# Key and query products stored once per direction, with a triangle cleared for each, in one layer of a gated DeltaNet and neighbourhood attention kernel

## The chip, the cores and the metric

The kernel runs on one core of one Trainium2 chip. The metric is the device time of one execution in microseconds (us). The engines are named as the profile names them: PE (TensorE matmul), PEld (its weight loads), DVE (VectorE), ACT (ScalarE), POOL (GpSimd) and SP (SyncE, which here issues the DMAs). Each has one instruction queue that it works through in order.

## The reference, cut to what matters

One layer: modulation, a combined input projection, a gated DeltaNet over 1280 tokens (256 of context, 1024 latent, 4 heads of 128), scanned once forward and once backward, beside a neighbourhood attention, an output projection and a SwiGLU. The part that the change concerns is what the scans need within a chunk:

```
gam = jnp.cumsum(g.astype(f32).reshape(B, H, n, CHUNK), axis=-1)
tril = jnp.tril(jnp.ones((CHUNK, CHUNK), dtype=bool))
strict = jnp.tril(jnp.ones((CHUNK, CHUNK), dtype=bool), -1)
decay = jnp.exp(jnp.where(tril, gam[..., :, None] - gam[..., None, :], -jnp.inf))
kb = k * beta[..., None]
m = jnp.where(strict, jnp.einsum("bhncd,bhnmd->bhncm", kb, k) * decay, 0.0)
...
qk = jnp.where(tril, jnp.einsum("bhncd,bhnmd->bhncm", q, k) * decay, 0.0)
...
o_b, S_b = chunk_gated_delta_rule(rev(q), rev(k), rev(v), rev(g[1]), rev(beta[1]), S0_b)
```

The products of keys with keys and of queries with keys are multiplied by a decay that holds in one triangle only: the lower one forward, the other one backward.

## The kernel before

The kernel works in chunks of 128 tokens: `NCH` = 10 chunks, of which the first two are context. It has stages one after the other: modulation from `wa` and the norms; the column blocks of the input projection (k, z, the attention's q, k and v, then v, z and q of the DeltaNet); in the middle of these the preparation of the scans; the scans and the attention; the output projection; and the FFN, whose 700 us (810 to the end) have nothing to do with the change.

A column block (class `Block`) is projected in three partial matmuls (L419: `hh,whi`, `hl,whi`, `hh,wlo`), convolved on DVE (L461 or L475) and normalised. Its method `finish` then makes the products. For k block i (head i) PE multiplies keys by keys, chunk by chunk, into PSUM, ACT copies them into the tile `kk` (L568, 128x1280), POOL multiplies `kk` by the identity into `kd` (L572), DVE sums that to the squared norms `SV` (L574), and POOL moves the 32x32 diagonal blocks out of `kk` (L577) and clears them (L578). SP then stores `kk` to `kk_d` in HBM (L580). For q block i `kT` is loaded back into `kTh`, PE multiplies it by the queries, ACT copies the products into a `kk` of 128x1024, and SP stores it to `qk_d`. `kk`, `kd`, `kTh` and the `vt` that holds a transposed block share one ring of three buffers (tag "kx"); ACT can fill one only when its earlier content is no longer needed.

The decays: DVE makes the tables (`decay_tables`: L806 to L840, ending in `G` and its halves `GH`, `GL`); PE takes sums over them (L848), which the later preparation (L871 on POOL, L884 on PE) needs too. It stands in DVE's queue around the fourth k block. In the preparation (`preps`, with `fetch` and `prep`), which runs beside the later column blocks, there are 10 iterations of two tiles each, one for each direction `d`. `fetch` loads `kk` from `kk_d`, and for latent chunks `at` from `qk_d`. POOL multiplies `GH` and `GL` by a triangle (L994, `rg`); PE sums these in a matmul with a triangle of ones, `mr[:, d]` (L1006); then a third matmul (L1009) of an identity `mr[:, 4]` with `mneg` adds −1e30 outside the triangle, so that ACT's exponential (L1014, `e`) is 0 there. DVE multiplies `kk` by `e` (L1017) and `at` by `e` (L1022); PE multiplies `kk` by the blocks `fx` (L1030), ACT copies, and then rounds of L1041 on PE with copies of `y` (L1043) follow.

The order of the instructions on the engines is set by a scheduler from the written program; some rows are kept in program order (L1008). The L223 matmuls sum the modulation products `acc`, which DVE accumulates in L238 from tiles `wad`.

## Time and profile before

| | us |
|---|---|
| median of 3 runs | 1509.69 (1507.06 to 1513.23) |
| the profiled execution | 1510.77 |
| its span | 1509.0 |
| PE busy | 1458.9 (97%) |
| DVE busy | 993.4 (66%) |
| ACT busy | 704.0 (47%) |
| POOL busy | 237.5 (16%) |
| mean granted TensorE clock | 0.996 |

A row of the timeline gives the start in us, the time that it takes (in a row with x2 or more, of all of them together), the engine, the line, the operation, what it writes and reads, and in brackets how long the engine sat idle before it and on what. A row of the groups gives the number, the busy time and the mean in ns. DMAs appear under SPq with the time that they take to issue; "landing" is the time from issue until the data has arrived.

### The profile page before, as it was taken

Reading aid. Unit: us, or ns where it says so; the run is one execution under the profiler, and the core shown is the slowest. Engines: PE = TensorE matmul, PEld = TensorE weight load, DVE = VectorE, ACT = ScalarE, POOL = GpSimd, SP = SyncE. Lnnn points to the kernel's source line nnn. Section 1 sums busy time; section 2 is a strip of 40 time slices with the busy share of each in tenths; the row PEclk is TensorE's granted clock in tenths of the full one; section 3 lists DMA queues with packets and bytes.
Section 4 is the critical chain, followed back from the end, with each engine's and each line's share of the span. In section 5 each row is a group of like instructions: output and inputs, shape, how many; then the busy total and the mean of one; then the engine's idle time right before and its main releaser. Section 6 shows DMA issues by size and latency. Waiting matters only on the chain.

```text
span 1509.0 us, 23906 instructions
## 1 busy us (share of the span) xinstructions
PE 1458.9 (97%) x8702; PEld 1222.2 (81%) x8702; DVE 993.4 (66%) x1716; ACT 704.0 (47%) x1389; POOL 237.5 (16%) x286
## 2 busy tenths in 40 slices
PE   6999999999999998999999999999999999999998
PEld 3788797877788887888878888888888888888887
DVE  5773589865463745779867489765555567598652
ACT  5443442456663246667843284333333334354440
POOL 1154501455652201112210000000000000000000
PEclk9999999999999999999999999999999999999999
DMA  9274132778665558999539205333333335798742
GB/s 385 79 220 138 57 83 64 248 211 248 189 195 185 157 164 289 300 261 293 166 119 338 76 28 174 134 105 105 105 105 105 105 105 174 271 349 279 251 140 84
DMA packets 205398, 267.36 MB, mean 177 GB/s; under 512 B 15968, under 2 KB 113760, under 8 KB 204256
## 3 DMA queue, kind: packets, MB, share of 16 engines
q1 hardware_dynamic: 197680, 260.01, 53.5%
q10 hardware_dynamic: 7600, 5.81, 1.2%
q8 instruction: 69, 1.13, 0.3%
q14 instruction: 49, 0.40, 0.1%
HBM read 201.02 MB, written 68.94 MB: 179 GB/s over the span
## 4 chain that ended last, share of the span: by engine, by line
PE 51%; ACT 1%; DVE 1%; issue 0%; DVEq 0%
PE ps L1404 28%; PE ps L1747 14%; PE ps L1533 3%; PE ps L1381 1%; PE ps L1555 1%; PE sc L322 1%; PE sc L332 1%; PE sc L309 1%; DVE bt L313 0%; ACT sq L1308 0%; PE ps L1258 0%; ACT oacc L1325 0%; PE ps L223 0%; PE ps L1279 0%; PE ps L1284 0%
## 5 line engine op out<-in xcount | busy, mean ns | idle before, releaser
L1465 ACT CAST uhi<-wq 128x512 fp32r<-128x512 f32 x101 | 61.3, 622 | 135.4 <-issue 84.6
L419 PE MATMUL blk<-hh,whi 128*128 128x512 f32 (+1 forms) x410 | 121.2, 389 | 1.5 <-ACT kk L568 1.4
L1465 ACT CAST uhi<-ws 128x512 fp32r<-128x512 f32 x91 | 53.9, 621 | 146.6 <-PE ps L1404 92.1
L615 PE MATMUL blk<-zw,hh 128*128 128x256 f32 (+1 forms) x576 | 113.2, 291 | 1.0 <-ACT cr L467 1.0
L419 PE MATMUL blk<-hl,whi 128*128 128x512 f32 (+1 forms) x410 | 113.4, 370 | 0.3 <-DVE hl L735 0.3
L419 PE MATMUL blk<-hh,wlo 128*128 128x512 f32 (+1 forms) x410 | 112.5, 371 | 0.6 <-POOL wlo L204 0.6
L1466 DVE TENSOR_TENSOR ulo<-wq,uhi 128x512 fp32r<-128x512 f32 x101 | 67.6, 687 | 59.1 <-ACT uhi L1465 32.8
L1404 PE MATMUL ps<-hT,uhi 128*128 128x512 f32 x336 | 103.7, 390 | 0.0
L1404 PE MATMUL ps<-lT,uhi 128*128 128x512 f32 x336 | 103.5, 389 | 0.0
L1404 PE MATMUL ps<-hT,ulo 128*128 128x512 f32 x336 | 103.4, 389 | 0.0
L615 PEld LDWEIGHTS blk<-zw,hh 128*128 128x128 f32 x576 | 91.5, 190 | 4.2 <-ACT cr L467 1.4
L1404 PE MATMUL ps<-hB,uhi 128*128 128x512 f32 x288 | 89.1, 390 | 0.0
L1404 PE MATMUL ps<-lB,uhi 128*128 128x512 f32 x288 | 88.8, 389 | 0.0
L1404 PE MATMUL ps<-hB,ulo 128*128 128x512 f32 x288 | 88.6, 389 | 0.0
L419 PEld LDWEIGHTS blk<-hh,wlo 128*128 128x128 f32 x410 | 71.2, 189 | 14.8 <-POOL wlo L204 0.9
L419 PEld LDWEIGHTS blk<-hl,whi 128*128 128x128 f32 x410 | 71.3, 189 | 14.3 <-DVE hl L735 0.8
L615 PE MATMUL blk<-zw,hl 128*128 128x256 f32 (+1 forms) x288 | 82.3, 286 | 0.0
L419 PEld LDWEIGHTS blk<-hh,whi 128*128 128x128 f32 x410 | 67.9, 190 | 16.7 <-issue 3.8
L204 POOL TENSOR_TENSOR wlo<-wraw,whi 128x1024 fp32r<-128x1024 f32 x18 | 44.8, 2491 | 185.1 <-ACT whi L203 178.8
L1404 PEld LDWEIGHTS ps<-lT,uhi 128*128 128x128 f32 x336 | 63.1, 188 | 13.2
L1404 PEld LDWEIGHTS ps<-hT,ulo 128*128 128x128 f32 x336 | 63.1, 188 | 13.1
L1404 PEld LDWEIGHTS ps<-hT,uhi 128*128 128x128 f32 x336 | 62.9, 188 | 12.9
(361 smaller groups left out, 3499.3 us busy)
## 6 DMA issues: line engine op xcount, KB each, us to landing
wq<-w_fo SPq DMA_DIRECT2D x99, 256.0 KB, 4.4
wq<-w_gu SPq DMA_DIRECT2D x88, 256.0 KB, 2.9
wad<-wa SPq DMA_DIRECT2D x64, 256.0 KB, 4.2
bt<-rpb SPq DMA_DIRECT2D x64, 192.0 KB, 4.0
t_d<-g SPq DMA_DIRECT2D x22, 512.0 KB, 3.5
fr<-t_d SPq DMA_DIRECT2D x44, 256.0 KB, 4.9
f_d<-g SPq DMA_DIRECT2D x33, 256.0 KB, 2.1
fr<-f_d SPq DMA_DIRECT2D x33, 256.0 KB, 4.4
```

The source lines that it names most:

```text
L204: lo_engine.tensor_tensor(o, r, h.bitcast(F32), OP.subtract)
L309: s = pe.matmul(sc[:, u * 640 + n0:u * 640 + n1], q, ks[i], start=i == 0, stop=i == 1)
L322: pe.transpose(sc[:, u * 640 + j * 128:u * 640 + (j + 1) * 128], bt[:, j * 128:(j + 1) * 128], ident)
L332: return pe.matmul(sc[u * ND:u * ND + ND, 1280:1408], vv, pts[u][:, j * 128:(j + 1) * 128], start=j == 0, stop=j == 4)
L419: pe.matmul(o, ww[:, k], xx[k][:, s], start=k == 0 and j == 0, stop=k == KT - 1 and j == 2)
L615: pe.matmul(p[:, :c1 - c0], x[k][:, s], ww[:, k, c0:c1], start=k == 0 and j == 0, stop=k == KT - 1 and j == 2)
L1381: pe.matmul(o, w[wi][:, k], parts[xi][k][:, s], start=k == 4 and j == 0, stop=k == 3 and j == 2)
L1404: pe.matmul(o, w[wi][:, k], x[xi][:, k], start=first and k == 0 and j == 0, stop=k == n - 1 and j == 2, skip_group_check=True)
L1465: act.copy(hi, self.raw[key])
L1466: dve.tensor_tensor(lo, self.raw[key], hi.bitcast(F32), OP.subtract)
L1533: pe.matmul(o, w[wi][:, k], parts[xi][k][:, s], start=k == 0 and j == 0, stop=k == KT - 1 and j == 2)
L1747: pe.matmul(o[b], w[wi][:, b], F[xn, p][xi], start=n in (0, 1, 5) and p == 0 and j == 0, stop=p == NFB // 2 - 1 and j == 2, skip_group_che ...
```

## The change

After the products of a block, DVE makes two masked copies of `kk`, one for each direction: `kk` times the triangle `M[C_LE + d]` into the tile that is free by then (`kd` for k, `kTh` for q), and then into `kk` itself. SP stores both, in HBM tensors with a leading dimension of 2 for the direction, and `fetch` loads those of its direction, as many bytes as before. With the products cleared outside the triangle, the third matmul of a preparation tile (L1009) goes, and with it `mneg` and the fifth slice of `mr`. That is 20 matmuls and 3 ACT operations less, 16 DVE multiplies and 8 stores of 640 or 512 KB more.

```diff
-    mr = const("mr", [128, 5, 128], F32R)
+    mr = const("mr", [128, 4, 128], F32R)
...
-    kk_d = dram.tile([128, NCH, 4, 128], F32, name="kk_d", tag="kk_d")
-    qk_d = dram.tile([128, 8, 4, 128], F32, name="qk_d", tag="qk_d")
+    kk_d = dram.tile([2, 128, NCH, 4, 128], F32, name="kk_d", tag="kk_d")
+    qk_d = dram.tile([2, 128, 8, 4, 128], F32, name="qk_d", tag="qk_d")
...
                     dst = kk_d if kind == "k" else qk_d
-                    sp.dma_start(dst[:, :, i], kk[:, c0:])
+                    other = kd if kind == "k" else kT.rearrange("p (c t) -> p c t", t=128)
+                    for d, x in enumerate((other, kk)):
+                        keep = M[C_LE + d].rearrange("p (o i) -> p o i", o=1).to_broadcast([128, NCH - c0, 128])
+                        dve.tensor_tensor(x[:, c0:], kk[:, c0:], keep, OP.mult)
+                        sp.dma_start(dst[d, :, :, i], x[:, c0:])
...
-                        act.copy(mr[:, 4], ident)
...
-        mneg = adp.tile([128, 2, 128], F32R, name="mneg", tag="mneg")
-        for d in range(2):
-            act.mul(mneg[:, d], mr[:, d].bitcast(F32), -1.0e30)
...
-                        sp.dma_start(kk, kk_d[:, c])
+                        sp.dma_start(kk, kk_d[d, :, c])
...
-                            sp.dma_start(at, qk_d[:, c - 2])
+                            sp.dma_start(at, qk_d[d, :, c - 2])
...
-                            m = pe.matmul(p, mr[:, d], fl(rgs[2 * d + j]), start=j == 0, stop=False)
+                            m = pe.matmul(p, mr[:, d], fl(rgs[2 * d + j]), start=j == 0, stop=j == 1)
                             if i == 0:
                                 tc.keep_in_program_order(m)
-                        pe.matmul(p, mr[:, 4], mneg[:, d].rearrange("p (o i) -> p o i", o=1).to_broadcast(
-                            [128, 4, 128]), start=False, stop=True)
```

In the changed file the masks are L583 and the stores L584; L1014, L1017, L1022, L1030, L1041 and L1043 become L1012, L1015, L1020, L1028, L1039 and L1041.

The scheduler puts the rows of the preparation in another order. Three places:

Place 1, DVE around the fourth k block (L574 is the sum of its squared norms; `gS`, `gE`, `gA`, `nA`, `B` are the decay tables, all 128x80 or smaller). Before:

```order
L574 TENSOR_REDUCE SV<-kd 128x10
L806 TENSOR_SCALAR nA<-nA 128x8
L815 TENSOR_SCALAR gS<-gE 128x80
L828 TENSOR_SCALAR B<-B 128x80
L816 RECIPROCAL gS<-gS 128x80
L829 RECIPROCAL B<-B 128x80
L817 TENSOR_TENSOR gS<-gS,gE 128x80
L832 TENSOR_SCALAR SV<-SV 128x40
L818 TENSOR_TENSOR gE<-gS 128x80
```

and now:

```order
L816 RECIPROCAL gS<-gS 128x80
L583 TENSOR_TENSOR kd<-kk,cst 128x1280
L817 TENSOR_TENSOR gS<-gS,gE 128x80
L583 TENSOR_TENSOR kk<-kk,cst 128x1280
L818 TENSOR_TENSOR gE<-gS 128x80
L829 RECIPROCAL B<-B 128x80
L819 TENSOR_SCALAR gP<-gE 128x80
L832 TENSOR_SCALAR SV<-SV 128x40
L821 SCALAR_TENSOR_TENSOR gP<-gP,gE 128x80
```

The two masks stand within the chain of tables, ahead of L818 and of everything that leads to `G`, and L829 has moved behind L818. On PE, the matmuls on `G` (L848) stood behind the k block's projection by `hh_452`, before:

```order
L419 MATMUL blk<-hl_453,whi 128x512 x2
L419 MATMUL blk<-hh_452,wlo 128x256
L419 MATMUL blk<-hh_452,wlo 128x512 x2
L848 MATMUL m<-G,cst 128x40
L848 MATMUL m<-G,mr 128x40
```

and now:

```order
L419 MATMUL blk<-hh_452,wlo 128x512 x2
L419 MATMUL blk<-hh_454,whi 128x256
L419 MATMUL blk<-hh_454,whi 128x512 x2
L419 MATMUL blk<-hl_455,whi 128x256
L419 MATMUL blk<-hl_455,whi 128x512 x2
L848 MATMUL m<-G,cst 128x40
```

Six L419 matmuls with `hh_454` and `hl_455` have moved from behind L848 to ahead of it.

Place 2, DVE around the first q block (`acc` with its number is the modulation sum, `wad` its tile). Before:

```order
L475 SCALAR_TENSOR_TENSOR cacc<-cr,cw,cacc 128x1022
L504 COPY SQ<-m 128x8
L238 SCALAR_TENSOR_TENSOR acc_2457<-wad,sc_100,acc_2457 128x512 x2
L225 TENSOR_TENSOR modp<-m,prm 128x4
L471 TENSOR_SCALAR cacc<-cr,cw 128x1024
```

and now:

```order
L504 COPY SQ<-m 128x8
L238 SCALAR_TENSOR_TENSOR acc_2465<-wad,sc_100,acc_2465 128x512
L583 TENSOR_TENSOR kTh<-kk,cst 128x1024
L238 SCALAR_TENSOR_TENSOR acc_2465<-wad,sc_100,acc_2465 128x512
L583 TENSOR_TENSOR kk<-kk,cst 128x1024
L471 TENSOR_SCALAR cacc<-cr,cw 128x1024
L225 TENSOR_TENSOR modp<-m,prm 128x4
```

The first mask stands between the two last L238 of a sum, the second behind them.

Place 3, PE and DVE at the first tile pair of the preparation. PE before, from the L500 sums to the first L1030:

```order
L500 MATMUL m<-ones,cr 128x1 x8
L419 MATMUL blk<-hh_135,whi 128x512 x2
L419 MATMUL blk<-hl_136,whi 128x512 x2
L419 MATMUL blk<-hh_135,wlo 128x512 x2
L419 MATMUL blk<-hh_452,whi 128x512 x2
L419 MATMUL blk<-hl_453,whi 128x512 x2
L1030 MATMUL pr<-fx_2491,kk 128x128 x4
```

and now, where L1028 is the old L1030:

```order
L419 MATMUL blk<-hh_135,wlo 128x512 x2
L419 MATMUL blk<-hh_452,whi 128x512
L1028 MATMUL pr<-fx_2499,kk 128x128 x4
L1028 MATMUL pr<-fx_2500,kk 128x128 x4
L1039 MATMUL pr<-y_2501,kk 32x32 x4
```

DVE there, before:

```order
L475 SCALAR_TENSOR_TENSOR cacc<-cr,cw,cacc 128x1023
L504 COPY SQ<-m 128x8
L475 SCALAR_TENSOR_TENSOR cacc<-cr,cw,cacc 128x1023
L1017 TENSOR_TENSOR kk<-kk,e 128x512 x2
L475 SCALAR_TENSOR_TENSOR cacc<-cr,cw,cacc 128x1022
```

and now, where L1015 is the old L1017:

```order
L475 SCALAR_TENSOR_TENSOR cacc<-cr,cw,cacc 128x1023
L504 COPY SQ<-m 128x8
L1015 TENSOR_TENSOR kk<-kk,e 128x512 x2
L475 SCALAR_TENSOR_TENSOR cacc<-cr,cw,cacc 128x1023
L238 SCALAR_TENSOR_TENSOR acc_2729<-wad,sc_100,acc_2729 128x512
```

One L475 has moved from ahead of the pair to behind it on DVE, and three L419 from ahead of it to behind it on PE.

A fourth place, at the first `at` tiles: SP issues two stores for the last q block, the second after both masks, and then the loads of `at` one by one, each after the store of its direction.

## The prediction

> **What bounds the kernel now.** I read the page's busy shares first, then busy time by stage, then the idle time of the matmul engine piece by piece, and last the rows of the other engines around each piece.
>
> ```profile
> PE 1458.9 (97%) x8702; PEld 1222.2 (81%) x8702; DVE 993.4 (66%) x1716; ACT 704.0 (47%) x1389; POOL 237.5 (16%) x286
> ...
> 95.00:160.00 65.00, 61.65 (x431) 56.57 (x430) 32.71 (x76) 26.43 (x60) 35.24 (x46) 1.00 0.48 144
> 285.00:365.00 80.00, 76.53 (x482) 62.77 (x481) 53.32 (x70) 45.88 (x82) 47.47 (x52) 0.96 0.81 246
> 810.00:1509.00 699.00, 695.16 (x3078) 574.73 (x3076) 453.29 (x716) 275.94 (x470) 0.00 (x0) 1.00 0.46 156
> ```
>
> The first row gives busy time per engine; the others give, for a stretch, PE, PEld, DVE, ACT and POOL, then the granted clock, the DMA share and GB/s. PE is busy for 97% of the span, and for 695 of the last 699 us, which no edit touches. So a matmul that goes is worth its pitch, and work added on DVE, ACT, POOL or SP is free until PE waits for it. In the two stretches with the k blocks and the q blocks (65 and 80 us) PE idles 3.35 and 3.47 us in all: there the price is decided, stall by stall.
>
> **The matmuls that go.** Twenty, with as many weight loads.
>
> ```profile
> L1009 PE MATMUL pr<-mneg,mr x20: 387/392/398, 296.0 to 473.9; 128*128 128x512 f32 x20
> ...
> 295.96 0.40 PE L1009 MATMUL pr<-mneg,mr 128*128 128x512 f32 x1
> 296.19 0.40 PE L1006 MATMUL pr<-rg,mr 128*128 128x512 f32 x1
> ```
>
> One lasts 392 ns, but the next matmul starts 0.23 us later (296.19 − 295.96), and PE is a stream there. So 20 x 0.23 = **−4.6 us**; the ends are 0 (all in time that PE would then wait) and 20 x 0.392 = 7.8. I take the pitch, since the stretch of these rows has no idle before them. The Trainium skill (TensorE: Matmul & The Clock Gate, Back-to-back issue gap) gives about 131 ns per N=512 matmul in a sustained stream with weight loads; by that the term would be −2.6 and the sum below 2.0 higher, an estimate from that page; the trace's 0.23 us disagrees with it and decides.
>
> The two multiplies that make `mneg`, one copy of `ident` and their SBUF go from ACT and from the setup: ACT is 47% busy, and PE's waits there are not for these; 0.
>
> **The masks added.** Sixteen DVE multiplies (8 of 128x1280, 8 of 128x1024), and eight more stores on SP. DVE and SP are in order, so what counts is what stands behind each. Four places matter.
>
> *Place 1, the fourth k block.* In the new order both masks stand on DVE ahead of most of the decay tables' chain, and the first mask waits for POOL's last clearing of `kk`. L848 on PE waits for the end of this chain (`G`).
>
> ```profile
> 145.42 0.77 POOL L578 MEMSET kk<- 32x320 f32 x2
> 149.53 1.04 POOL L871 TENSOR_TENSOR rc<-GH,cst 128x512 fp32r<-128x512 f32 x1 [3.34 <-DVE gY L835]
> ...
> 145.04 0.59 DVE L829 RECIPROCAL B<-B 128x80 f32<-128x80 f32 x1
> 145.76 0.24 DVE L818 TENSOR_TENSOR gE<-gS 128x80 f32<-128x80 f32 x1
> ...
> 286.77 1.47 DVE L941 TENSOR_TENSOR WK<-WK,NB 128x1280 f32<-128x1280 f32 x1
> ...
> 149.10 0.41 PE L848 MATMUL m<-G,cst 128*128 128x40 f32 x2 [0.42 <-DVE G L827]
> ...
> 150.46 0.83 PE L419 MATMUL blk<-hh,whi 128*128 128x256 f32 x3
> 151.71 0.74 PE L419 MATMUL blk<-hh,wlo 128*128 128x256 f32 x3
> ```
>
> The clearing ends at 145.42 + 0.77 = 146.19. A mask is a two-operand multiply of 128x1280 f32, as L941 is: 1.47 us. Two of them, and the small L817 between them, end at 146.2 + 2 x 1.47 + 0.1 = 149.2. From L818 to PE's start at L848 it takes 149.10 − 145.76 = 3.34, and the new order moves L829 (0.5 of it not overlapped, 145.55 − 145.04) behind L818, while one or two small table steps of under 0.2 go behind `G`: +0.3. So L848 can start at 149.2 + 3.34 + 0.3 = 152.85. PE now has six more L419 ahead of L848; the rows at 150.46 and 151.71 bracket just six: 1.25. It would arrive at 149.10 − 0.42 + 1.25 = 149.93 and wait 2.9 us instead of 0.42: **+2.5**. Ends: +1.0 (were the two masks to cost together one row) and +6.5 (each as dear as the dearest two-operand row of that size on DVE, 3.48, quoted with the rivals). POOL idles 3.34 us after 146.19, until `GH` exists (row at 149.53), so I take 1.47. The L871 and L884 work behind follows `GH`, 2.5 us later too, with PE equally late: 0.
>
> *The ring of k tiles.* `kk`, `kd` and `vt` share three buffers. `kd` was free as soon as DVE had reduced it; now it must have landed in HBM before ACT may evacuate the next block's products into that buffer, and ACT waits in order.
>
> ```profile
> DMA to landing us min/median/max: 2.7/4.1/6.2
> ...
> 116.28 0.52 SPq L580 DMA_DIRECT2D kk_d<-kk  x1
> 130.06 0.53 SPq L580 DMA_DIRECT2D kk_d<-kk  x1
> ...
> 120.42 0.59 ACT L568 COPY kk<-m 128x512 f32<-128x512 f32 x1 [1.09 <-DMA kk_d<-kk]
> 122.59 0.86 ACT L568 COPY kk<-m 128x512 f32<-128x512 f32 x2 [0.34 <-PE m L567]
> 138.24 1.33 ACT L568 COPY kk<-m 128x512 f32<-128x512 f32 x3
> ...
> 139.63 0.85 PE L419 MATMUL blk<-hh,whi 128*128 128x256 f32 x3 [1.40 <-ACT kk L568]
> ```
>
> The first row is the landing of the four `kk_d` stores. The second block's masked `kd` is ready at 116.28 + 1.47 = 117.8, so the third block's first copy may start at 117.8 + 4.1 = 121.9 instead of 120.42; its third copy ended at 122.59 + 0.86 = 123.45 for want of PE's products, and 121.9 + 1.57 for the three copies is as early: 0. The third block's `kd` lands at 130.06 + 1.47 + 4.1 = 135.7, before the fourth block's copy at 138.24: 0. With a landing of 6.2 the third block is 117.8 + 6.2 + 1.57 − 123.45 = 2.1 late, its store lands at 139.9, and 1.6 is added to the 1.40 that PE waits at 139.63. I take **+0.4**, ends 0 and 1.6.
>
> *Place 2, the first q block.* The new order has the 128x1024 mask of `kTh` between the two L238 that L223 waits for.
>
> ```profile
> 289.45 1.52 DVE L238 SCALAR_TENSOR_TENSOR acc<-wad,sc,acc 128x512 f32<-128x512 f32 x2
> ...
> 362.91 1.27 DVE L516 SCALAR_TENSOR_TENSOR cacc<-cacc,qkw,cr 128x1024 f32<-128x1024 f32 x1
> ...
> 291.11 1.02 PE L223 MATMUL m<-ones,acc 128*128 128x1 f32 x8 [1.16 <-DVE acc L238]
> ```
>
> The nearest 128x1024 row with two tensors takes 1.27, some 0.1 to 0.2 of it overlapped with its neighbours: **+1.1**, ends 0.9 and 2.2, all on PE's 1.16 us wait.
>
> *Place 3, the first decay preparation.* PE waits there for L1017, which stands on DVE behind an L475.
>
> ```profile
> 299.78 2.74 DVE L475 SCALAR_TENSOR_TENSOR cacc<-cr,cw,cacc 128x1023 f32<-128x1023 f32 x1
> 302.45 2.97 DVE L1017 TENSOR_TENSOR kk<-kk,e 128x512 f32<-128x512 f32 x2
> ...
> 301.46 0.63 PE L419 MATMUL blk<-hl,whi 128*128 128x512 f32 x2
> 304.02 1.16 PE L1030 MATMUL pr<-fx,kk 128*128 128x128 f32 x8 [1.94 <-DVE kk L1017]
> 305.56 0.97 PE L1030 MATMUL pr<-fx,kk 128*128 128x128 f32 x5 [0.38 <-DVE kk L1017]
> ```
>
> In the new order the L475 comes after the pair, and PE has three L419 fewer before L1028 (the old L1030). PE came at 304.02 − 1.94 = 302.08; it comes 3 x 0.23 earlier, two removed matmuls (0.46) earlier, and 1.1 later by place 2: 302.03. The pair starts where the L475 did, at 299.78 + 1.1 − 0.46 = 300.4, and at 2.97 for both ends at 301.9 and 303.4. PE does 0.5 us of the first half and waits about 0.8, against 1.94 + 0.38 = 2.32: **−1.5**, ends −2.3 and 0.
>
> *Place 4, the first `at` tiles.* Their load waits for the fourth q block's store.
>
> ```profile
> 351.91 0.56 SPq L580 DMA_DIRECT2D qk_d<-kk  x1
> 356.90 1.27 SPq L982 DMA_DIRECT2D at<-qk_d  x3
> ...
> 354.34 2.14 DVE L1017 TENSOR_TENSOR kk<-kk,e 128x512 f32<-128x512 f32 x2 [3.44 <-ACT e L1014]
> 360.26 2.73 DVE L1022 TENSOR_TENSOR at<-at,e 128x512 f32<-128x512 f32 x2 [3.78 <-DMA at<-qk_d]
> ...
> 366.20 0.64 PE L1041 MATMUL pr<-y,kk 128*32 128x64 f32 x16
> ```
>
> The masks fall into the 3.44 us in which DVE idles before 354.34, but the second direction's store goes out near 355.2 instead of 351.91, so that direction's `at` comes at about 363.4 instead of 360.26. The DVE work behind it (one L1022 half of 2.73, an L516 of 1.27) ends near 366.0, and the copy of `y` that PE's 366.20 row needs is then about 0.6 late: **+0.6**, ends 0 and 2. The masks of the q blocks between find DVE idle and nothing of PE behind: 0, at most +0.5. Later order differences move small DVE and SP rows by a few places: ±3 in the range.
>
> **The clock.** A short stall can also open a half-clock window.
>
> ```profile
> 306.10:309.50 3.40, 3.40 (x18) 0.51 0.01 2
> ...
> 570.18 1.16 PE L1267 MATMUL ps<-v,y 128*128 128x128 f32 x8 [2.42 <-DMA y<-y_d]
> 568.00:570.00 2.00, 0.00 (x0) 1.00 0.97 356
> ```
>
> After the 2.32 us at place 3 the granted clock is 0.51 for 3.4 us (a loss of 1.7); after the 2.42 us before 570.18 it stays 1.00. So length alone doesn't decide it. Place 1's longer wait may open a window (+1.7), and place 3's shorter one may close its own (−1.7): 0, ends ±1.7. The Trainium skill (TensorE: Matmul & The Clock Gate, The HAM clock gate) asks for an idle window of some 3.4 us before the clock halves; by that rule place 1 adds nothing, and the window at 306 should not be there; the trace has it and disagrees.
>
> **Sum.** −4.6 + 2.5 + 0.4 + 1.1 − 1.5 + 0.6 = −1.5: 1510.77 (the profiled execution) − 1.5 = 1509.3. That execution lies 1.1 above the median of the runs shown, 1509.69; against the median: **1508.2**.
>
> **Rivals.**
>
> *The gain is kept.* Place 3's whole 2.32 us and its window go, and place 2's mask costs nothing because the second L238 waits for something else as long: −1.5 − 0.8 − 1.7 − 1.1 = −5.1, 1504.6 against the median. For it: both terms rest on fractions of a microsecond in an order that has moved. Against: L223 waited for DVE and not for a transfer.
>
> *The ring blocks ACT (slower).* Two stores of 640 KB now go out close together where one did. If the masked `kd` takes as long to land as another transfer of that size:
>
> ```profile
> xt<-xcT SPq DMA_DIRECT2D x8, 640.0 KB, 9.0
> ...
> L891 DVE TENSOR_TENSOR W<-W,NB 128x1280 f32<-128x1280 f32 x1 | 3.5, 3477 | 9.0 <-ACT W L886 9.0
> ```
>
> At 9.0 us the third block is 117.8 + 9.0 + 1.57 − 123.45 = 4.9 late, its `kd` lands at 131.5 + 4.9 + 9.0 = 145.4, and PE's wait at 139.63 grows by 145.4 − 138.24 = 7.2, with a clock window 1.7: −1.5 − 0.4 + 7.2 + 1.7 = +7.0, 1516.7. It decides from the landing at which 131.5 + 2L − 4.1 passes 138.24: L = 5.4. For it: ACT is in order and has PE's evacuations behind that copy. Against: DMA moves 144 GB/s in this stretch, 246 in the q stretch, and at least two of the four landings above are under 5.4. The second row is a two-operand multiply of a mask's size that took 3.48 us, with POOL at work on the `rc` tiles; masks that slide until POOL works beside them would bring place 1 to its dear end.
>
> *No stall at all*: only the matmuls count, −4.6, 1505.1. It would need `G` not to wait for the masks, against the order: part of the first rival's chance.
>
> **From cases to numbers.** Forecast 0.6 (its own range 1504 to 1513: the ends of places 1 to 4 and one window either way), gain kept 0.22, ring 0.18. A change under 0.5% (7.5 us) is about what timing cannot tell from none: 1502.1 to 1517.2. Of the kept gain some two in five lie below it, with the run spread of 2.6 to 3.5 us on either side of the median: faster 0.10; of the ring half, and a little of the forecast: slower 0.12; same 0.78. Range 1502 to 1517.
>
> **What would show it.** Each step: no `mneg` rows; L848 waiting about 2.9 us for DVE `G`; L223 waiting about 2.3; L1028 waiting under 1 in place of 2.3; the L568 copies waiting for `kk_d<-kd` without PE's L419 wait passing 1.8; PE busy less by 4.6 us with the last 699 us unchanged. I am wrong if L848 waits no longer than before (the masks were elsewhere), if the masks take 2 us or more beside POOL, or if a wait of PE shows up at a place not listed.

## The result, and the profile after

The changed kernel is slower: 1527.05 us median of 4 executions (1522.45 to 1529.73) against 1510.40 (1507.06 to 1513.23), a ratio of 1.0109 with a 95% interval of 1.0090 to 1.0127. The forecast was 1508.2, with 1502 to 1517 as the range and a chance of 0.12 for slower. The execution that was profiled took 1529.73 us, 18.96 more than the one profiled before.

The page of the changed kernel, its busy shares, and the same stretches as before the change (columns: PE, PEld, DVE, ACT, POOL busy, granted clock, DMA share, GB/s):

```profile
PE 1466.3 (96%) x8682; PEld 1227.7 (80%) x8682; DVE 1015.2 (66%) x1732; ACT 704.2 (46%) x1387; POOL 241.6 (16%) x286
...
95.00:160.00 65.00, 56.52 (x395) 52.61 (x393) 39.98 (x74) 21.30 (x49) 29.20 (x40) 0.96 0.62 187
285.00:365.00 80.00, 73.70 (x468) 61.57 (x467) 63.73 (x73) 36.46 (x61) 40.07 (x38) 0.96 0.76 234
```

PE has 20 matmuls less and is busy 7.4 us longer; it is idle 61.6 us instead of 50.1. The sixteen masks (L583) take 26.6 us on DVE; DVE's busy time is 21.8 us longer in all. In the k stretch PE idles 8.5 us instead of 3.35, and the granted clock there is 0.96 instead of 1.00.

PE's main waits in the change's region, from its timeline (start, duration, row, idle before it and its releaser):

```profile
109.48 0.39 PE L619 MATMUL blk<-zw,hh 128*128 128x272 f32 x1 [2.96 <-ACT kk L568]
157.82 0.41 PE L848 MATMUL m<-G,cst 128*128 128x40 f32 x2 [4.12 <-DVE G L827]
305.48 1.84 PE L223 MATMUL m<-ones,acc 128*128 128x1 f32 x8 [3.80 <-ACT fx L998]
320.96 0.44 PE L1039 MATMUL pr<-y,kk 128*32 128x32 f32 x8 [0.86 <-POOL y L1018]
334.48 1.16 PE L1028 MATMUL pr<-fx,kk 128*128 128x128 f32 x8 [1.05 <-DVE y L1041]
374.75 1.05 PE L223 MATMUL m<-ones,acc 128*128 128x1 f32 x8 [0.95 <-ACT cr L509]
441.86 0.64 PE L1039 MATMUL pr<-y,kk 128*32 128x32 f32 x8 [2.34 <-ACT kk L1031]
456.46 1.16 PE L1028 MATMUL pr<-fx,kk 128*128 128x128 f32 x8 [1.88 <-DVE y L1041]
```

Three of its waits before the change, beside those that the prediction shows:

```profile
98.10 0.44 PE L543 MATMUL m<-cst,cacc 128*128 128x128 f32 x2 [1.54 <-DVE cacc L461]
428.99 0.64 PE L1041 MATMUL pr<-y,kk 128*32 128x64 f32 x16 [1.92 <-DVE y L1043]
437.69 1.16 PE L1030 MATMUL pr<-fx,kk 128*128 128x128 f32 x8 [0.48 <-DVE y L1043]
```

The waits in the k stretch moved about when the same changed kernel was profiled a second time (e15 below), PE and then ACT:

```profile
111.35 0.40 PE L619 MATMUL blk<-zw,hh 128*128 128x272 f32 x1 [1.20 <-ACT kk L568]
145.28 0.86 PE L419 MATMUL blk<-hh,whi 128*128 128x256 f32 x3 [2.86 <-ACT kk L568]
159.71 0.47 PE L848 MATMUL m<-G,cst 128*128 128x40 f32 x2 [2.65 <-DVE G L827]
...
143.88 1.35 ACT L568 COPY kk<-m 128x512 f32<-128x512 f32 x3 [1.35 <-DMA kk_d<-kd]
```

In the first profile the L419 and L848 behind the fourth k block wait 1.40 and 4.12, in the second 2.86 and 2.65: the sum, 5.5 us, is the same, and before the change it was 1.8. So one wait of one profile is good to 1 to 2 us, and sums over a stage are safer.

Where the 18.9 us of the two spans lie, between the same rows of both programs (idle is length less PE's busy time):

| from, to | before | change | more | of it PE idle |
|---|---|---|---|---|
| 20 us, first product of a k block | 60.9 | 61.6 | 0.7 | −0.2 |
| to the first L848 | 68.2 | 76.2 | 8.0 | 5.1 |
| to the first product of a q block | 132.1 | 135.1 | 3.0 | −0.1 |
| to the first L1006 | 13.6 | 17.4 | 3.8 | 2.6 |
| to the last L1041 (now L1039) | 194.7 | 195.8 | 1.1 | 3.5 |
| to the first FFN matmul on `hT` | 401.6 | 403.9 | 2.3 | 0.4 |
| to the end | 617.9 | 617.9 | 0 | 0 |

In the fifth row lie the removed matmuls: PE's busy time there fell by 2.5 us (189.4 to 187.0) and its idle time rose by 3.5. What idle time does not explain is the clock. Stretches of 3.4 us at half clock, each a loss of up to 1.7 us of PE's work, were 3 before and are 11 now: 13.6 us in this pair of profiles.

### The profile page after: what moved, and what is told of

The parts are those of the page before. It is cut to its first block, busy times and chain, and to the rows that moved or that the text cites. A ratio compares the mean times of both kernels' runs of the same rounds, so it can differ in the third digit from the quotient of the medians.

```text
span 1527.9 us, 23906 instructions
## 1 busy us (share of the span) xinstructions
PE 1466.3 (96%) x8682; PEld 1227.7 (80%) x8682; DVE 1015.2 (66%) x1732; ACT 704.2 (46%) x1387; POOL 241.6 (16%) x286
## 3 DMA queue, kind: packets, MB, share of 16 engines
q8 instruction: 68, 1.11, 0.3%
## 4 chain that ended last, share of the span: by engine, by line
PE 58%; DVE 2%; DMA 2%; ACT 2%; issue 1%; SPq 0%; POOL 0%; DVEq 0%; POOLq 0%; ACTq 0%
PE ps L1402 28%; PE ps L1745 14%; PE ps L1531 3%; PE sc L332 2%; PE sc L322 2%; PE blk L619 2%; PE sc L309 2%; PE ps L1379 1%; PE ps L1553 1%; PE ps L1265 1%; PE ps L1246 1%; PE ps L1282 1%; DVE bt L313 1%; DMA bt<-rpb 1%; PE ps L1256 1%
## 5 line engine op out<-in xcount | busy, mean ns | idle before, releaser
L419 PE MATMUL blk<-hh,whi 128*128 128x512 f32 (+1 forms) x410 | 123.0, 393 | 1.4 <-ACT kk L568 1.4
L619 PE MATMUL blk<-zw,hh 128*128 128x256 f32 (+1 forms) x576 | 114.8, 293 | 5.2 <-ACT kk L568 3.0
L419 PE MATMUL blk<-hl,whi 128*128 128x512 f32 (+1 forms) x410 | 115.3, 375 | 0.3 <-DVE hl L739 0.3
L419 PE MATMUL blk<-hh,wlo 128*128 128x512 f32 (+1 forms) x410 | 114.9, 376 | 0.6 <-POOL wlo L204 0.6
L619 PEld LDWEIGHTS blk<-zw,hh 128*128 128x128 f32 x576 | 92.8, 193 | 8.7 <-ACT kk L568 3.2
L419 PEld LDWEIGHTS blk<-hl,whi 128*128 128x128 f32 x410 | 72.5, 191 | 14.7 <-DVE hl L739 0.8
L419 PEld LDWEIGHTS blk<-hh,wlo 128*128 128x128 f32 x410 | 72.4, 192 | 14.9 <-POOL wlo L204 0.9
L619 PE MATMUL blk<-zw,hl 128*128 128x256 f32 (+1 forms) x288 | 83.1, 288 | 0.0
L419 PEld LDWEIGHTS blk<-hh,whi 128*128 128x128 f32 x410 | 68.8, 193 | 16.8 <-issue 3.8
L204 POOL TENSOR_TENSOR wlo<-wraw,whi 128x1024 fp32r<-128x1024 f32 x18 | 45.0, 2502 | 181.2 <-ACT whi L203 181.0
```

Source lines behind the costliest of these rows:

```text
L204: lo_engine.tensor_tensor(o, r, h.bitcast(F32), OP.subtract)
L419: pe.matmul(o, ww[:, k], xx[k][:, s], start=k == 0 and j == 0, stop=k == KT - 1 and j == 2)
L619: pe.matmul(p[:, :c1 - c0], x[k][:, s], ww[:, k, c0:c1], start=k == 0 and j == 0, stop=k == KT - 1 and j == 2)
```

## The experiments

Theory A, held ahead of e1, was that the masks and their stores make PE wait, and that these waits open half-clock stretches; theory B that any new order of the rows opens stretches at waits that were there all along. After e1 to e4 theory A became A': such a stretch follows where PE idles for about half of a window of a fixed 3.41 us grid or more. Lines in an experiment's rows are its own and differ by a few from those of the change.

Span times mean granted clock, averaged over a kernel's executions, is taken as its time without the clock's loss; span times (1 − clock) is that loss. The clock is reported to three digits, so one execution is good to 0.75 us and a mean over four or more to some tenths. The loss is an upper measure: among executions of the same kernel (198, pooled), 1 us more of it went with 0.76 us more time, so about three quarters of a difference in that column are a difference in time. The last two rows of the table are the changed kernel.

| run | median us | before beside it | ratio, 95% interval | clock loss | without it |
|---|---|---|---|---|---|
| kernel before (19 executions beside e15) | 1510.22 | | | 5.6 | 1502.4 |
| e1 matmuls out, no masks | 1513.75 | 1509.96 | 1.0024 (1.0015 to 1.0034) | 8.2 | 1503.5 |
| e2 k masks only | 1525.50 | 1509.96 | 1.0102 (1.0087 to 1.0117) | 14.9 | 1508.8 |
| e3 q masks only | 1518.07 | 1509.96 | 1.0054 (1.0039 to 1.0069) | 10.6 | 1505.8 |
| e4 kd in its own buffer | 1520.67 | 1509.96 | 1.0072 (1.0056 to 1.0089) | 11.0 | 1508.1 |
| e5 two multiplies in the tables | 1513.56 | 1510.86 | 1.0014 (0.9997 to 1.0030) | 6.7 | 1504.9 |
| e6 e4, k masks behind the tables | 1517.85 | 1510.86 | 1.0049 (1.0032 to 1.0065) | 11.2 | 1505.8 |
| e7 e6, q masks behind the sum | 1517.12 | 1510.86 | 1.0043 (1.0028 to 1.0058) | 9.9 | 1505.6 |
| e8 e1, first y copies on ACT | 1510.67 | 1510.86 | 0.9998 (0.9984 to 1.0012) | 7.1 | 1501.8 |
| e9 e4, idle matmuls at L848 | 1522.92 | 1510.64 | 1.0078 (1.0053 to 1.0104) | 9.9 | 1511.0 |
| e10 e6, L223 in program order | 1521.96 | 1510.64 | 1.0079 (1.0054 to 1.0103) | 13.7 | 1507.1 |
| e11 before, L223 in program order | 1510.46 | 1510.64 | 0.9999 (0.9986 to 1.0013) | 6.8 | 1501.7 |
| e12 e8, L223 in program order | 1514.63 | 1510.64 | 1.0018 (1.0004 to 1.0033) | 9.8 | 1502.2 |
| e13 e3 without the multiplies | 1512.58 | 1510.22 | 1.0018 (1.0007 to 1.0029) | 8.8 | 1501.8 |
| e14 change without the multiplies | 1510.97 | 1510.22 | 1.0017 (1.0002 to 1.0032) | 8.8 | 1502.1 |
| change, first four | 1527.05 | 1510.40 | 1.0109 (1.0090 to 1.0127) | 15.3 | 1509.5 |
| e15 change again | 1528.40 | 1510.22 | 1.0131 (1.0105 to 1.0156) | 17.6 | 1509.6 |

**e1: the matmuls alone.** Edit against the kernel before:

```diff
-                            m = pe.matmul(p, mr[:, d], fl(rgs[2 * d + j]), start=j == 0, stop=False)
+                            m = pe.matmul(p, mr[:, d], fl(rgs[2 * d + j]), start=j == 0, stop=j == 1)
-                        pe.matmul(p, mr[:, 4], mneg[:, d].rearrange("p (o i) -> p o i", o=1).to_broadcast(
-                            [128, 4, 128]), start=False, stop=True)
```

(and `mneg` and `mr[:, 4]` with it)

> The kernel before without the 20 L1009 matmuls and without mneg, and with no masks and no second store (so the triangles are not cleared: that part of the computation is left out). Theory A (the loss comes from stalls that the masks and their stores cause, and from half-clock windows that those stalls open): nothing new waits, so 20 x 0.23 = 4.6 us less than before, about 1506, with two to four half-clock windows. Theory B (any new order of the rows shifts the phase of the clock, and windows open at stalls that were there all along): six or more windows, 1512 to 1520, although no stall of PE is over 2.5 us after 95 us.

Slower by 0.24%: no gain, though nothing was added. Theory A's 1506 missed; the time lies in theory B's range, but not B's sign, since a new long wait is there and half-clock stretches are five. Without the clock it is 1.1 to 1.4 us above before. Its profile shows one long wait that the kernel before doesn't have, and the POOL rows that explain it:

```profile
308.30 0.64 PE L1035 MATMUL pr<-y,kk 128*32 128x32 f32 x8 [3.83 <-POOL y L1014]
...
304.56 2.02 POOL L990 TENSOR_TENSOR rg<-GH,cst 128x512 fp32r<-128x512 f32 x1
306.53 1.48 POOL L990 TENSOR_TENSOR rg<-GL,cst 128x512 fp32r<-128x512 f32 x1
307.96 4.51 POOL L1014 COPY y<-xc 32x128 f32<-32x128 f32 x12
```

The scheduler put the second direction's L1035 earlier on PE, and there it meets POOL's copy of `y` behind four `rg` multiplies. The matmuls are gone, and PE waits for POOL in their place.

**e2 and e3: the k masks alone, the q masks alone.** In e2 the q block is stored once, unmasked:

```diff
+                    if kind == "q":
+                        sp.dma_start(dst[0, :, :, i], kk[:, c0:])
-                    for d, x in enumerate((other, kk)):
+                    for d, x in enumerate((other, kk) if kind == "k" else ()):
...
-                            sp.dma_start(at, qk_d[d, :, c - 2])
+                            sp.dma_start(at, qk_d[0, :, c - 2])
```

and e3 is the same with k and q exchanged.

> The changed kernel with the k blocks' masks and stores, but the q products stored once and unmasked (the q triangle is not cleared: left out). Theory A: the loss up to 270 us stays: PE waits about 3 us at the L619 behind the second k block, and about 4 us at L848, each with a window; the wait at the L223 behind the first q block falls back from 3.8 to about 1.2. Some 1516 to 1521. Theory B: 1520 to 1528, no clear link to the masks.

> The changed kernel with the q blocks' masks and stores, but the k products stored once and unmasked (the k triangle is not cleared: left out). Theory A: L848 waits under 1 us and the L619 wait at 109 us is gone; L223 behind the first q block waits about 3.8 us with a window. Some 1508 to 1514. Theory B: 1518 to 1528.

Both lose, and both times lie above theory A's range and inside or at the edge of theory B's; the waits are at theory A's places, though not in its sizes. In e2 PE waits 1.22 at the L619 behind the second k block, 2.91 at the L419 behind the fourth and 2.63 at L848 (its L850), as in the second profile of the change, and 1.14 at L223; in e3 L848 is not among the waits over 0.45 us, and L223 waits 2.94. Against the matmuls alone (e1) the k masks cost 11.8 us and the q masks 4.3; with e1's own 3.8 that makes 19.9, against 16.7 for the whole. The split is rough, because e1's wait for POOL's `y` is in e2 too (2.83) and not in e3 (0.9): against e8, which lacks it, the q masks cost 7.4.

**e4: the ring.** The whole change, with one line else:

```diff
-                        kd = cp.tile([128, NCH, 128], F32, name="kd", tag="kx", bufs=3)
+                        kd = cpa.tile([128, NCH, 128], F32, name="kd", tag="kd", bufs=1)
```

> The whole change, with kd in a buffer of its own in place of the ring of three (it computes everything). Theory A, ring part: ACT's copies of kk no longer wait for a store or for k_d, so the 3.0 us wait at 109 us is gone with its window, POOL's multiply into kd no longer waits for a kk store, and L848 waits about 2.9 us as forecast instead of 4.1; 5 to 8 us less than the changed kernel, 1519 to 1522. If the ring plays no part (rival: only the masks' own time on DVE counts): 1525 to 1529, L848 still 4 us.

6.4 us less than the change, the middle of what was expected; by the means, the last column falls by 1.4 and the clock's by 4.3. The wait at 109 us is gone and L848 waits what the prediction had, with the six L419 ahead of it as the prediction had them:

```profile
151.96 0.65 PE L848 MATMUL m<-G,cst 128*128 128x40 f32 x2 [2.90 <-DVE G L827]
```

**e5: place 1 by itself.** The kernel before, with two idle multiplies in the chain:

```diff
-            dve.tensor_tensor(E, S, S, OP.mult)
+            dve.tensor_tensor(D, sb, sb, OP.mult)
+            dve.tensor_tensor(D, D, D, OP.max)
+            dve.tensor_copy(E.rearrange("p d c h -> p (d c h)"), D[:, 0])
```

`D` has 128x1280 elements, `sb` is `S` repeated sixteen times.

> The kernel before, with nothing of the change, but with two extra 128x1280 multiplies on DVE inside the decay tables' chain, just ahead of L818 (they compute nothing new). It prices place 1 by itself: the chain is some 2.9 us longer and PE has eight L419 (1.7 us) more ahead of L848. Theory A': a stall of S costs S plus one or two half-clock windows of 3.4 us (1.7 us each) when it takes more than about half of a window of a fixed 3.41 us grid: L848 waits about 1.7 us longer in its place (1.5 to 3), with a window in some executions: +2 to +5 us, 1512 to 1515. Rival (the clock has nothing to do with such stalls): +1.5 to +2.5, no window after L848. Rival of a hidden cost: no change.

2.7 us more at the median, an interval that just includes none: as expected in size, but unclear as a verdict. L848 waited 1.79 us in the profile, and one half-clock stretch lay behind it (154.7 to 158.2).

**e6 and e7: the masks moved.** e6 is e4 with the fourth k block's masks and stores issued after the instruction that makes `GL`; e7 also puts the first q block's masks behind the last L238 of the sum:

```diff
+                    def put(other=other, kk=kk, dst=dst, i=i, c0=c0):
...
+                    if kind == "k" and i == 3:
+                        puts.append(put)
...
             for _ in range(4):
                 yield
+            while puts:
+                with tc.issue_after(gl.ins):
+                    puts.pop()()
```

> The whole change, kd in its own buffer, and the fourth k block's masks put behind the decay tables on DVE (computes everything). Theory A': L848's wait of 2.9 us falls below 0.6 and its two half-clock windows go: 2.4 + 1.7 to 3.4 less than with kd's buffer alone (1520.7), so 1515 to 1517. Rival (the masks only move: the L891 and L893 work behind the tables becomes late and PE waits at L906 or L928 instead): 1519 to 1521.

> As the run before, and the first q block's masks also put behind the last L238 of the sum that L223 reads (computes everything). Theory A': L223's wait falls from 3.7 us to 1.2 to 2 with at most one window: another 2 to 5 us less, 1511 to 1515. Rival (nothing of the order of the masks matters, POOL's rg multiplies are what DVE shares time with): L223 still waits 3 us, 1515 to 1517.

e6 takes 2.8 us off e4 and is where the q masks alone are (1517.85 and 1518.07): with the ring and place 1 mended, the k side costs nothing more that these intervals could show, though the fall is less than theory A' had (1515 to 1517). e7 takes off another 0.7, which the intervals don't tell from none; L223 still waits 2.62 us. Theory A' missed there, and the rival (L223 still waits, 1515 to 1517) has it within 0.2 us.

**e8: e1 with another engine for one copy.**

```diff
-                            pool.tensor_copy(y[d][q, :, q], xc[q, 0])
+                            (act.copy if i == 0 else pool.tensor_copy)(y[d][q, :, q], xc[q, 0])
```

> The kernel before without the 20 L1009 matmuls and without masks (the triangles are not cleared: left out), as in the first run, but with the first iteration's copies into y on ACT in place of POOL. In the first run PE waited 3.8 us for POOL's copy, which stood behind four rg multiplies, with a double half-clock window behind it. Theory A': this wait falls under 1 us and the windows go with it: 4 to 7 us less than 1513.75, 1507 to 1510, so that the 4.6 us of the matmuls begin to show against the kernel before. Rival (the wait passes to another row, ACT or DVE, of the same length): 1512 to 1515.

The wait for `y` is gone and 3.1 us with it, less than the 4 to 7 expected; the kernel stands level with before. The L1024 now waits 1.93 us for DVE's `kk`, which the two L1030 rows of before did too (2.32).

**e9: the same wait, filled.** e4 with 30 matmuls that nobody reads ahead of L848:

```diff
             pg = bank()
+            for _ in range(30):
+                tc.keep_in_program_order(pe.matmul(pg[:, 256:512], mr[:, 0], mr[:, 0:2].rearrange("p a b -> p (a b)"),
+                                                   start=True, stop=True))
```

> The whole change with kd in its own buffer, and 30 matmuls of 256 columns that nobody reads (about 3.5 us of PE) just ahead of L848, where PE would wait some 4 us (the six L419 stand behind L848 here). Theory A' (a half-clock window is opened by PE's idle time within a window of a fixed 3.41 us grid): the wait is as long, but filled, so no window of the clock behind L848; with kd's buffer alone two of them lay there (151.7 to 158.5), 3.4 us. 1516 to 1518 against 1520.7. Rival (the windows are chance or follow from something else than idle PE): windows still there, 1520 to 1523.

At the place itself it went as the clock theory has it. Three windows of 3.4 us around L848, first of e4, then of e9 (PE busy, granted clock, DMA share, GB/s):

```profile
148.20:151.60 3.40, 0.86 (x5) 1.00 0.97 285
151.60:155.00 3.40, 3.04 (x14) 0.51 0.34 94
155.00:158.40 3.40, 3.40 (x11) 0.50 0.00 0
```

```profile
148.20:151.60 3.40, 3.40 (x29) 1.00 0.78 234
151.60:155.00 3.40, 2.90 (x22) 1.00 0.51 154
155.00:158.40 3.40, 3.40 (x18) 1.00 0.00 0
```

With PE busy through the wait there is no half-clock stretch behind it. From the first L848 to the first q product e9 takes 132.5 us and e4 134.5. The total did not follow: 1522.92, within the rival's numbers. The L848 comes 0.7 later, L223 waits 4.58 us instead of 3.73, and three more half-clock stretches fell elsewhere. So the run shows, at one place, that a filled wait leaves the clock alone, and not that this pays.

**e10 to e12: L223 in program order.** One edit, on e6, on the kernel before, and on e8:

```diff
-                pe.matmul(p[:, b:b + 1], acc2[:, b * 128:(b + 1) * 128], ones[:, 0:1], start=True, stop=True)
+                m = pe.matmul(p[:, b:b + 1], acc2[:, b * 128:(b + 1) * 128], ones[:, 0:1], start=True, stop=True)
+                if bufs == 3 and q == 1:
+                    tc.keep_in_program_order(m)
```

> The whole change (it computes everything) with kd in its own buffer, the fourth k block's masks behind the decay tables, and the four L223 matmuls of the sum at the first q block kept in program order on PE, some 5 us later. Theory A': neither L848 nor L223 waits over 0.6 us, and their windows are gone; against 1517.9 without the last edit 2.9 us of wait and one or two windows less: 1511 to 1514. Rival (another wait takes the place, at the first L1028 or y copies): 1516 to 1518.

> The kernel before, with only the four L223 matmuls kept in program order on PE. Theory A': the 1.16 us wait at 291 and, in executions where it opened one, its half-clock window go: 1 to 3 us less, 1507 to 1510. Rival (the scheduler's early place cost nothing since PE waits for the same DVE work at L1030): no change.

> The kernel before without the 20 L1009 matmuls and without masks (triangles not cleared: left out), the first iteration's y copies on ACT, and the L223 matmuls kept in program order: the run before this one with the matmuls taken away, so the two give the worth of the matmuls alone. If they are worth their pitch: 4.6 us less than that run, about 1503 to 1505. Rival (PE's time there is refilled by waits for DVE and POOL, which set the pace of the preparation): the same as that run within 1.5 us.

No gain came in any of the three. e11 is its rival's "no change". e10 and e12 came out dearer than their rivals' numbers too (1521.96 against 1516 to 1518, and 4.2 us above e11 where 1.5 were allowed), but with what the rivals said would happen: the wait passes to other rows. In e10 the L223 wait is gone and these stand in its place:

```profile
301.56 0.50 PE L1016 MATMUL pr<-rg,mr 128*128 128x512 f32 x1 [1.24 <-POOL rg L1004]
305.97 1.16 PE L1038 MATMUL pr<-fx,kk 128*128 128x128 f32 x8 [1.39 <-DVE kk L1025]
309.11 1.16 PE L1038 MATMUL pr<-fx,kk 128*128 128x128 f32 x8 [1.75 <-DVE kk L1025]
```

e11 and e12 differ only by the matmuls and the engine of the first y copies, and price the matmuls. The stretch from the first of the `rg` sums to the last round on `y`, of e11 and then of e12:

```profile
293.30:489.00 195.70, 190.34 (x1438) 158.08 (x1439) 108.41 (x136) 111.87 (x225) 106.40 (x128) 0.99 0.70 215
```

```profile
292.50:488.40 195.90, 186.21 (x1419) 154.00 (x1419) 110.54 (x136) 113.24 (x233) 105.85 (x120) 0.99 0.70 214
```

PE's busy time falls by 4.1 us, near the forecast 4.6, and the stretch is as long: 195.7 and 195.9. PE idles 9.7 us instead of 5.4. Most of the 4.3 us more is one place in e12, which e11 doesn't have (behind it 0.38 more, on the same tile):

```profile
302.75 1.16 PE L1026 MATMUL pr<-fx,kk 128*128 128x128 f32 x8 [2.82 <-DVE kk L1013]
```

Without the clock's loss e11 takes 1501.7 and e12 1502.2. e12's median is 4.2 us above e11's; 3.0 of them are in the clock's column.

**e13 and e14: the stores without the multiplies.** e3 and the change, each with one line less:

```diff
-                        dve.tensor_tensor(x[:, c0:], kk[:, c0:], keep, OP.mult)
```

> As the run with the q masks alone, but with the eight q multiplies left out: both tiles are still held and stored (no triangle is cleared: left out). If DVE's time for the q masks is the loss: back to the matmuls alone, 1512 to 1514, L223 waits under 2 us. If the stores, the buffers or the other order are: 1516 to 1519.

> The whole change with all sixteen mask multiplies left out: kd and kk, kTh and kk are stored as they are (no triangle is cleared: left out). The ring still holds every tile until its store has landed. If the masks' time on DVE is the main loss (place 1 and place 2): L848 waits under 1 us, L223 under 2, 1513 to 1517. If the ring is: PE still waits about 3 us at the L619 behind the second k block, and POOL's multiply into kd still waits for a store; 1518 to 1523.

This settles what of the change costs. e13 is what was expected if DVE's time is the loss, and e14 came out below the lower of its two ranges. With both stores and the ring as they are, but the sixteen multiplies gone (so nothing is cleared), e14's loss is 0.17%, no more than with the matmuls alone. L848 is not among the waits over 0.45 us, and L223 waits 1.82. The multiplies and what they hold up are worth 16 to 17 us: about 7.5 in the last column and the rest in the clock's. The ring's share is in this: it costs only where the masks delay the stores. The second stores by themselves are not seen. For theory B this leaves little: three kernels whose rows are in a new order, but without masks' time (e1, e13, e14), lose 8 to 9 us to the clock against some 6 before, and at most 0.24% in all.

**e15: the change again.**

> The changed kernel once more, to see whether its clock loss repeats. Theory A' (long stalls open half-clock windows in nearly every execution): mean clock 0.988 to 0.993 in most executions against 0.994 to 0.998 before, 1522 to 1529. Rival (the first four executions fell badly on the clock's grid): mean clock near 0.995, 1516 to 1520.

1526.54 to 1532.54, mean clock 0.986 to 0.990: the clock's loss repeats, as theory A' had it and its rival not. Over both sets it is 16.4 us against some 6 before.

## Why the prediction was wrong, point by point

Three steps failed. The clock was put at 0 because the length of a wait seemed not to decide; it cost about 10 us of lost clock, some 8 us of the 17. The removed matmuls were priced at their pitch, −4.6; three kernels without them, and without masks, were no faster than before (e1, e8, e12). The ring was put at +0.4; it added about 2.5 us of PE's waits. Place 1 came out as worked out, and waits at rows that the prediction had not listed added some 3 us.

**The masks at place 1** (+2.5). The price of the masks and the chain was right, as e4 shows with its 2.90 against the forecast 2.9. In the change itself the wait was 4.12, because POOL allocates from the ring too. Rows of the change, POOL and then DVE:

```profile
129.80 2.95 POOL L572 TENSOR_TENSOR kd<-kk,cst 128x1280 f32<-128x1280 f32 x1 [11.55 <-DMA kk_d<-kk]
144.72 2.95 POOL L572 TENSOR_TENSOR kd<-kk,cst 128x1280 f32<-128x1280 f32 x1 [8.43 <-DMA kk_d<-kk]
...
151.23 1.49 DVE L583 TENSOR_TENSOR kd<-kk,cst 128x1280 f32<-128x1280 f32 x1 [1.11 <-POOL kk L578]
154.19 0.23 DVE L818 TENSOR_TENSOR gE<-gS 128x80 f32<-128x80 f32 x1
157.57 0.31 DVE L827 TENSOR_TENSOR G<-gA,nA 128x40 f32<-128x40 f32 x2
```

POOL's multiply into `kd` waits for the second store of the block before, whose buffer it takes; ACT had the fourth block's `kk` ready at 143.4 (142.08 + 1.33 for its three copies), so 1.3 us went there. In the second profile L848 waits 2.65, but only because PE had lost as much at the L419 ahead of it. The prediction asked who waits on ACT for the ring, and not who else allocates from it. Its sign of being wrong, masks of 2 us or more beside POOL, came up once among the k masks: the very first took 3.07 us (100.47) while POOL ran an L204, the other seven 1.5.

**The ring** (+0.4, ends 0 and 1.6). Mis-sized. Behind the fourth k block the change waits 5.5 us in both profiles and e4 4.3, so the ring has 1.2 there. Around the second, L543 and L619 together wait 2.96 and 2.69 in the two profiles, against 1.54 before and 1.64 in e4: 1.1 to 1.4 more. That is about 2.5 us, and 6.4 in all with the clock (e4). The wait at 109.48 stands on an ACT copy behind a `k_d` store:

```profile
108.84 1.07 ACT L568 COPY kk<-m 128x512 f32<-128x512 f32 x2 [0.82 <-DMA k_d<-vt]
```

With `kd` and `kk` both held until their stores land, the next `kk` takes the buffer of `vt`. The prediction followed the third and fourth blocks and took the second as safe. It also read the landings wrongly: 2.7/4.1/6.2 is over the stores and loads of `kk_d` together. The four stores before the change land in 3.9 to 4.0; of the change's eight, those of the first two blocks land in 6.4 to 7.7 and the later ones in 4.0 to 5.1. Its ring rival asked for over 5.4 us at two blocks in a row and got 6.5 at one: ACT's wait for `kd`, and 1.46 us more of PE's at the L419, are in the second profile and not in the first.

**Place 2** (+1.1, ends 0.9 and 2.2): 2.64 in the first profile, beyond the dear end, and 1.8 in the second (2.96 against 1.16) and in e3, within it. The profile names ACT as the releaser in the first, but L223 starts 0.15 us after the last L238 in both. The rows of the first:

```profile
301.83 2.06 DVE L583 TENSOR_TENSOR kTh<-kk,cst 128x1024 f32<-128x1024 f32 x1
303.81 1.52 DVE L238 SCALAR_TENSOR_TENSOR acc<-wad,sc,acc 128x512 f32<-128x512 f32 x1
...
302.77 2.02 POOL L994 TENSOR_TENSOR rg<-GL,cst 128x512 fp32r<-128x512 f32 x1
```

and the same two of e6, whose first `rg` row starts at 294.07:

```profile
292.16 1.22 DVE L584 TENSOR_TENSOR kTh<-kk,cst 128x1024 f32<-128x1024 f32 x1
293.29 0.74 DVE L238 SCALAR_TENSOR_TENSOR acc<-wad,sc,acc 128x512 f32<-128x512 f32 x1
```

The mask takes 2.06 us beside POOL's `rg` multiplies, and the L238 behind it 1.52; without them they take 1.22 and 0.74. In the second profile the first `rg` row starts after the mask has (304.28 against 303.93), and only the L238 is slow (1.21 and 1.52). The Trainium skill (GPSIMD Engine Reference, Specifications) says that GpSimd shares its SBUF interface with VectorE and contends with DVE instructions of two SBUF inputs; these rows agree. The prediction used that price for the k masks as a rival and not here, where POOL's four `rg` multiplies stood in the timeline of before from 290.63 on, just behind.

**Place 3** (−1.5): right. The waits of 1.94 and 0.38 are gone, and 0.86 for POOL's `y` at 320.96 is there: −1.46.

**Place 4** (+0.6): no wait at the `y` copy; instead 0.95 us at the L223 at 374.75, on ACT, which e14 without any mask has as well (1.00). That the size is near is luck.

**Places not listed.** At 334.48 PE waits 1.05 us for a copy of `y` that stands on DVE behind the second q block's first mask:

```profile
332.63 1.22 DVE L583 TENSOR_TENSOR kTh<-kk,cst 128x1024 f32<-128x1024 f32 x1
333.88 0.55 DVE L1041 COPY y<-pr 32x384 f32<-32x384 f32 x1
```

The wait is in the second profile (1.03) and not in e14. The prediction had nothing of PE behind the q blocks between, at most 0.5.

At 441.86 and 456.46 PE waits 2.34 and 1.88 us, where before it waited 1.92 and 0.48. ACT's rows there:

```profile
440.18 1.14 ACT L528 CAST hl<-cacc 128x512 f16<-128x512 f32 x2 [2.65 <-DVE cacc L516]
441.23 0.58 ACT L1031 COPY kk<-pr 128x512 f32<-128x512 f32 x1
```

The second L1031 stands behind an L528 that waits for DVE; before, both copies came ahead of it. The run without any multiply (e14) has the same pair, 2.31 and 1.88, so this is the order of the rows and not the masks' time.

**The matmuls** (−4.6). The step that failed is "a matmul that goes is worth its pitch". PE is 97% busy over the span, but in the preparation it is one of several engines that take turns: e11 and e12 show 4.1 us less work and as long a stretch. In e1 and e12 a new wait in the first preparation takes the time back, on another row each time: 3.83 for POOL's `y`, 2.82 for DVE's `kk`. e8 bounds the gain from the other side: the matmuls gone, nothing added, no new wait over 2 us in the preparation, and the time is that of before within 0.16%. Its profile is 2.6 us shorter than before's from the first q product to the last round on `y` (205.7 against 208.3) and 1.7 longer from there to the first FFN matmul. So a part of the pitch can be had in the stage; nothing of it reached the end. Since every edit also brought another order of the rows, no run takes the matmuls out with all else in place.

**The clock** (0, ends ±1.7). The largest miss: about 10 us more lost (16.4 against 6), some 8 us of the 17 to 18 at 0.76 for each. The matmul rows bear the granted clock out: L848's start 0.11 us apart up to 158.18, where a half-clock stretch begins, and 0.21 behind it. In all seventeen profiles the half-clock stretches after the first begin at whole multiples of 3.4133 us from it, within 0.014 of a multiple, 66 of 66. On that grid, for windows at full clock between 24 and 850 us, the next window was at half clock in 27 of 27 cases with 2.0 us or more of PE idle, in 34 of 49 with 1.6 to 2.0, in 10 of 203 with 0.9 to 1.6, and in 4 of 3717 below. It was followed by a second one in 11 of 11 cases with 2.6 us or more, and in none with less. Idle time is not quite the measure: in the 4 windows PE was busy throughout, but for 1.5 to 2.4 us with sums of one column each (128x1, as in L223). With these rows counted as idle, it is 35 of 35 from 2.0 us on and none of 3640 below 0.9. Two such places of the change:

```profile
154.80:158.20 3.40, 0.38 (x4) 1.00 0.96 284
158.20:161.60 3.40, 3.40 (x16) 0.50 0.11 32
161.60:165.00 3.40, 3.40 (x11) 0.50 0.00 0
301.50:304.90 3.40, 0.18 (x1) 1.00 0.81 224
304.90:308.30 3.40, 2.82 (x11) 0.51 0.90 258
308.30:311.70 3.40, 3.40 (x10) 0.50 1.04 326
```

So length does decide, once it is counted within the grid: of 17 waits of 2.6 us or more in these profiles 16 had a half-clock window right behind them, and at both places above two in a row; the one without (2.82 in e12) the grid split into 1.54 and 1.28. The many waits of 1 to 1.5 us open one now and then, by where the grid falls. The prediction read one 2.32 us wait with a window and one 2.42 us wait without, and took that as chance for any length: the grid splits the 2.42 into 1.11 and 1.31, and has 1.78 us of the other in one window. A part of the 13.6 us in the two profiles is such chance: the stretch at 28 us lies ahead of the first mask (100.5). That idle time opens the window was tested once by filling a wait (e9); for the rest it is this count. The Trainium skill (TensorE: Matmul & The Clock Gate, The HAM clock gate) calls the activity window free-running and about 3.4 us long: the grid agrees. It gives a whole idle window as the condition for half clock; here 2 us of 3.4 were enough each time, so the trace disagrees.

**What stays open.** Why the q masks' cost (4 us over e1) did not go when they were moved (e7): L223 still waits 2.62 us there, and each edit gave another order of rows. No version with the change was faster than the kernel before: the best that leaves nothing out is e7, 0.43% slower.

## What to carry to other kernels

An engine that is 97% busy over a span can still be paced by others in one stage; price a removed instruction by the idle time around it in that stage, and try it alone before paying for it. Where work is added on an in-order engine, list everyone who waits for its outputs and for its buffers, on every engine that allocates from the same ring, and use the price beside the neighbours that will be running then. Count a new wait of PE of 3 us as up to 4.7 to 6.4, since the clock follows it (one or two windows here, each up to 1.7). Profile a kernel twice before a single wait of it is priced.

## What the runs showed that was not expected

The clock's grid and its condition, above, and that sums of one column count there like idle time. Beside it: the masks' two stores (some 4.7 MB more written, by eight stores of 640 or 512 KB) cost nothing that could be measured, although the DMA queues moved 234 GB/s in the q stretch; and 26.6 us of masks on an engine that was busy 66% of the time cost 16 to 17 us, about half of it by PE's clock.
